# A decoder trunk layer on one core: stick-breaking scores as three products of float32r parts, with the norm weights' load and the squares moved

## The chip, the core and the metric

The kernel runs on one core of one Trainium2 chip. The metric is the device time of one execution in microseconds (us). The time before is 767.2 us, the median of three runs (766.13 to 767.41).

The names below are those of the profile. PE is the matrix engine, and PEld its loading of stationary operands; DVE, ACT and POOL are the vector, scalar and general engines; SP issues transfers. Each engine works through its own instructions strictly in the order in which the program holds them, and waits where an operand is not there yet.

## The reference

One layer with 512 tokens of 1024 features. Two token mixers read the same normalised input: stick-breaking attention (8 heads of 64) and a dilated sliding-window attention (12 heads of 64). Their outputs are projected up, gated, merged and projected out; a SwiGLU block with 2816 hidden features and a final norm follow. All of it is float32.

```python
u = rms_norm(x, norm_mix_g)
q_sb, k_sb, v_sb, q_dl, k_dl, v_dl, gate_sb, gate_dl = split(u @ w_in)
# stick-breaking, per head
z = (q @ k.T) / 8
log_keep  = where(causal, log_sigmoid(-z), 0)
log_after = reverse_cumsum(log_keep) - log_keep
a = where(causal, exp(log_sigmoid(z) + log_after), 0)
o_sb = a @ v
merged = sigmoid(gate_sb) * (o_sb @ w_sb_up) + sigmoid(gate_dl) * (o_dl @ w_dil_up)
x = x + merged @ w_out
u2 = rms_norm(x, norm_ffn_g)
x = x + (silu(g_ff) * up_ff) @ w_ffn_out      # g_ff, up_ff = split(u2 @ w_ffn_in)
out = rms_norm(x, norm_final_g)
```

## The kernel before

Features lie on the partitions and tokens along the free axis. Every large product is made of three: an operand is split into a float32r part (`hi`, a cast on ACT) and what the cast left over (`lo`, a subtraction on DVE), and `mm3` (L157) adds hi by hi, hi by lo and lo by hi into one bank. Weights come in chunks of 128 by 1024 from HBM on SP's queue (`dma_chunk`, L104) into a ring of three `raw` tiles, are split (`split_chunk`, L116) into `whi` and `wlo`, and are used two chunks later. `weights(i, ahead)` (L146) issues the transfers and the splits up to two chunks ahead of the product that asks.

**Start (L197 to L231).** Chunks 0 and 1 (query and key of the first pair of heads) and the eight tiles of x come in pieces, in turn. For each of the eight blocks k, `norm_split` (L175) multiplies x by the norm's weight `gt` on ACT (`xh`) and forms the rest on DVE (`xl`). `gt` is loaded on POOL's queue (L173). The four squares of x (L226) are held behind the last of these splits. The sixteen triples called `first` (L606) use the blocks as they come. Chunk 2 and the three that follow are the values, whose product is `pvvs`; chunk 2 uses blocks 0 and 1 alone.

**Attention.** Projections run on PE one after another; each is evacuated from its bank by DVE (`proj_feature`, L344), which multiplies by the row factors `rb`. There are two banks for projections (tag `proj`), used in turn, so the projection after next waits for the evacuation of this one. The attention's own work is written as generators that advance by ticks, one tick for each triple, and so lies between the projections: `sb_pair` (L412) for the four pairs of stick-breaking heads, with the score tiles `z0x`, `z0y`, `z0z` and so on for pair 0, and `dil_pair` (L507) for the two pairs of dilated heads. The scores of a pair are float32 products over the 64 features of a head, one head on the upper half of the partitions and one on the lower (L417). After the scores come the mask, the exponentials and the products with the values. `split_out` (L397) splits what a pair puts out into `oh` and `ol` tiles: `ohs`, `ols` for stick-breaking heads, `ohd`, `old` for dilated ones.

**What sets the order.** A scheduler that runs while the program is built decides the order on each engine; `tc.high_priority()` raises what lies in it. Tiles of one tag share a ring of buffers, which are handed out in the order in which the program asks for them. Before, the evacuated projections have the tag `qk` (16 buffers), the first four outputs tags of their own, and the two dilated outputs the tag `st` (4 buffers).

**After the attention** come the up projection, the gates (`gs`, `gd`, sixteen projections already made during the attention), the output projection and the SwiGLU block, whose PE order is written by hand. The change doesn't touch them.

Of the kernel before, what the change touches and what calls it, by code (L numbers as in the profile page):

```python
# [10 lines left out]
F32 = mybir.dt.float32  # L11
F32R = mybir.dt.float32r
# [4 lines left out]
P = 128  # L17
# [6 lines left out]
NEG = -(2.0 ** 100)  # L24
NOSYNC = mybir.DependencyInfo(mybir.DependencyClass.NoSync, mybir.DependencyReason.SCHED_ONLY)
BANKS = {"proj": 2, "att": 3}
RAW, NQ, N4, N2, NS = 3, 16, 9, 6, 4

HALVES = [0, 4, 1, 5, 2, 6, 3, 7]

# [13 lines left out]
def trunk_kernel(ctx, tc, xT, gains, w_in, w_up, w_o, w_f, w_d, bias, out):  # L44
# [20 lines left out]
    def bank(tag, name):  # L65
# [3 lines left out]
            return ppool[1].tile([P, S], F32, tag="att" if tag == "alpha" else "sums", name=name, bufs=BANKS["att"])  # L69
        return pair(name)[:, 0, :]  # L70


    warm = cp.tile([P, P], BF16)
    V.memset(warm, 0.0)
# [41 lines left out]
    def split_chunk(i):  # L116
        kind, _, n = chunks[i]
        if i < len(chunks) - 1 and i != first_s4:
            hi = wp.tile([P, 1024], F32R, tag="whi", name=f"whi{i}")
            lo = wp.tile([P, 1024], F32R, tag="wlo", name=f"wlo{i}")  # L120
        else:
            pair_ = wide(f"w{i}", F32R)
            hi, lo = pair_[:, 0, :], pair_[:, 1, :]
        parts[i] = (hi, lo)
        hi, lo = hi[:, :n], lo[:, :n]
        if kind == "plain":
            r = raws.pop(i)[:, :n]
        elif kind == "A1":
            r = raws[i]
        elif kind == "S23":  # L130

            u = raws[i]
            V.tensor_tensor(out=u[:, 0, :], in0=u[:, 1, :], in1=u[:, 2, :], op=ALU.add)
            r = raws["S23"] = wide(f"s23{i}")
            V.tensor_tensor(out=r, in0=u[:, 0:2, :], in1=raws[i - 1][:, :S].unsqueeze(1).to_broadcast([P, 2, S]), op=ALU.add)
        elif kind == "S1":
            r = raws.pop(i - 1)[:, 0:3:2, :]
        else:
            r = fpool[0].tile([P, S], F32, tag="s4", name=f"s4{i}", bufs=1)
            V.tensor_tensor(out=r, in0=raws["S23"][:, 0, :], in1=raws.pop(i - 3)[:, S:], op=ALU.add)  # L140
        if kind in ("S23", "S1"):
            hi, lo = (t.rearrange("p (a n) -> p a n", a=2) for t in (hi, lo))
        A.copy(hi, r)  # L143
        V.tensor_tensor(out=lo, in0=r, in1=hi.bitcast(F32), op=ALU.subtract)  # L144
# [17 lines left out]
    def split_to(hi, lo, src):  # L162
        A.copy(hi, src)
        return V.tensor_tensor(out=lo, in0=src, in1=hi.bitcast(F32), op=ALU.subtract)
# [3 lines left out]
    sqp = ctx.enter_context(tc.tile_pool(name="sqp", bufs=2))  # L168

    fpool = [None]  # L170
    gt = cp.tile([P, 24], F32)
    g32 = cp.tile([P, KD], F32)
    nc.gpsimd.dma_start(out=gt, in_=gains)  # L173

    def norm_split(k, x, gcol, hi, lo):  # L175
        g = gt[:, gcol + k:gcol + k + 1]
        i = A.mul(hi, x, g)
        V.scalar_tensor_tensor(out=lo, in0=x, scalar=g, in1=hi.bitcast(F32), op0=ALU.mult, op1=ALU.subtract)
        return i
# [33 lines left out]
    for k in range(KD):  # L213
        cs = slice(k * P, (k + 2) * P)
        if k % 2 == 0:
            split_to(parts[0][0][:, cs], parts[0][1][:, cs], raws[0][:, cs])
        hi = xp.tile([P, S], F32R, tag=f"xh{k}", name=f"xh{k}")
        lo = xp.tile([P, S], F32R, tag=f"xl{k}", name=f"xl{k}")
        last_split = norm_split(k, xw[k // 2][:, k % 2, :], 0, hi, lo)
        if k % 2 == 0:  # L220
            split_to(parts[1][0][:, cs], parts[1][1][:, cs], raws[1][:, cs])
        xh.append(hi)
        xl.append(lo)
    with tc.high_priority():
        for x in xw:
            i = A.activation(x, x, AF.Square)  # L226
            tc.add_manual_dep(i.ins, last_split.ins.name, NOSYNC, reason="issue order")
        V.tensor_tensor(out=xw[0], in0=xw[0], in1=xw[1], op=ALU.add)
        V.tensor_tensor(out=xw[2], in0=xw[2], in1=xw[3], op=ALU.add)
        V.tensor_tensor(out=xw[0], in0=xw[0], in1=xw[2], op=ALU.add)  # L230
        V.tensor_tensor(out=acc1, in0=xw[0][:, 0, :], in1=xw[0][:, 1, :], op=ALU.add)  # L231
# [109 lines left out]
                with tc.high_priority():  # L341
                    between[k]()

    def proj_feature(name, scale=None, ps=None, blocks=False):  # L344
        if ps is None:
            ps = bank("proj", f"pj{name}")
            product(ps, xh, xl, next_weights(), KD)
        rb = rows["rb"]
        o = ap_.tile([P, S], F32, tag="qk", name=name, bufs=NQ)
        view = (lambda t, out=False: t.rearrange("p (c i) -> p i c" if out else "p (i c) -> p i c", c=4)) if blocks else (lambda t, out=False: t)  # L350
        with tc.high_priority():
            if scale is None:
                V.tensor_tensor(out=view(o, True), in0=view(ps), in1=view(rb), op=ALU.mult)
            else:
                V.scalar_tensor_tensor(out=view(o, True), in0=view(ps), scalar=scale, in1=view(rb), op0=ALU.mult, op1=ALU.mult)
        return o

    def proj_token(name, kind, wide_, pairs=0):
# [36 lines left out]
    o_hi, o_lo = {}, {}  # L395

    def split_out(i, name, src):  # L397
        if i < 4:
            hi = ap_.tile([P, S], F32R, tag=f"oh{name}", name=f"oh{name}")
            lo = ap_.tile([P, S], F32R, tag=f"ol{name}", name=f"ol{name}")  # L400
        else:
            hi, lo = (ap_.tile([P, S], F32R, tag="st", name=f"o{t}{name}", bufs=NS) for t in "hl")
        split_to(hi, lo, src)
        o_hi[i], o_lo[i] = hi, lo

# [6 lines left out]
    def sb_pair(n, q, k, v, hb, done):  # L412
        def scores(name, parts):
            ps = take(f"z{n}{name}")
            for i, (a, o) in enumerate(parts):
                for h in range(2):
                    T.matmul(ps[:, h, o:o + S - a * P], k[hs[h], a * P:(a + 1) * P], q[hs[h], a * P:], start=i == 0, stop=False, skip_group_check=True)  # L417
            for h in range(2):
                diag = ps[:, h, :].rearrange("p (a b) -> p a b", b=P)
                diag = diag[:, 0:4:3, :] if len(parts) == 2 else diag[:, 0:1, :]  # L420
                T.matmul(diag, idb, mask[:, :len(parts)], start=False, stop=False, skip_group_check=True)
            return ps
# [165 lines left out]
            yield from dil_pair(n, [vals[f"dq{n}{g}"] for g in range(3)], [vals[f"dk{n}{g}"] for g in range(3)], lambda: vals.get("vd"))  # L588

    def project(n):  # L590
        vals[f"q{n}"] = proj_feature(f"sq{n}", 0.125)
        vals[f"k{n}"] = proj_feature(f"sk{n}")

    def project_dil(n):
        for g in range(3):
# [12 lines left out]
    def first_steps():  # L608
        yield from row_steps()
        give(3)  # L610
        vals["q0"] = proj_feature("sq0", 0.125, first[0])
        vals["k0"] = proj_feature("sk0", None, first[1])

    start(first_steps(), 10)
    start(sb_all())
# [384 lines left out]
```

## Time and profile before

| what | before |
|---|---|
| median of three runs | 767.2 us (766.13 to 767.41) |
| the profiled execution | 768.07 us |
| its span, first to last instruction | 766.4 us |
| granted PE clock, mean over the span | 0.995 |
| DVE busy | 511.6 us (67%) |
| ACT busy | 358.6 us (47%) |
| POOL busy | 29.0 us (4%) |
| HBM read | 71.32 MB |

The profiled execution lies 0.87 us above the median of the runs, and its span is 1.67 us shorter than its own time. Rows of the timeline read: start in us, duration in us, engine, line, operation, written tile, read tiles, shapes, count, and in brackets the idle time of that engine just before the row with what ended it. A float32r matmul over 512 columns is shown as 0.39 us long, but the next one starts 0.23 us after it, since they overlap; so starts count on PE, not durations.

### The profile page before, as it was taken

How to read it: one execution, taken by the hardware profiler on the slowest of the kernel's cores; microseconds unless marked ns; L12 is line 12 of the kernel's file. 1: busy time of each engine (PE TensorE's matmuls, PEld its weight loads, DVE VectorE, ACT ScalarE, POOL GpSimd, SP SyncE). 2: the span in 40 equal slices, each digit the busy share in tenths (PEclk: the TensorE clock that was granted, in tenths of full speed). 3: DMA queues.
4: the chain of work that ended last, by engine and by line, in shares of the span. 5: the costliest groups of instructions: out<-in, count | busy, mean ns of one | idle time of the engine just before them, and what ended most of it. 6: DMA issues, size and time to landing. Idle time of an engine off the chain costs nothing. (4 is left out here: it accounts for less than half of the span.)

```text
span 766.4 us, 11025 instructions
## 1 busy us (share of the span) xinstructions
PE 753.4 (98%) x4498; PEld 646.6 (84%) x4498; DVE 511.6 (67%) x685; ACT 358.6 (47%) x509; POOL 29.0 (4%) x38
## 2 busy tenths in 40 slices
PE   8999999999999999999999999999999999999996
PEld 5877767798887878888788999999999999999985
DVE  6454646344677775358698989877788777776643
ACT  7273727462233352333455666544445454444453
POOL 1000000000101100000000100000000000000032
PEclk9999999999999999999999999999999999999998
DMA  7312121123224223233432223323333323332113
GB/s 247 137 56 83 56 83 56 56 69 124 83 83 159 88 84 103 62 91 129 145 103 79 75 89 103 103 79 122 98 106 114 103 82 113 100 105 77 56 55 111
DMA packets 24947, 74.13 MB, mean 97 GB/s; under 512 B 2736, under 2 KB 5824, under 8 KB 24768
## 3 DMA queue, kind: packets, MB, share of 16 engines
q1 hardware_dynamic: 23664, 69.87, 28.3%
q0 software_dynamic: 816, 3.16, 1.3%
q8 instruction: 35, 0.57, 0.3%
q10 hardware_dynamic: 416, 0.39, 0.2%
q14 instruction: 16, 0.13, 0.1%
HBM read 71.32 MB, written 2.10 MB: 96 GB/s over the span
## 5 line engine op out<-in xcount | busy, mean ns | idle before, releaser
L143 ACT CAST whi<-raw 128x1024 fp32r<-128x1024 f32 (+2 forms) x113 | 108.5, 962 | 160.8 <-issue 49.2
L144 DVE TENSOR_TENSOR wlo<-raw,whi 128x1024 fp32r<-128x1024 f32 (+2 forms) x113 | 125.9, 1115 | 34.4 <-ACT whi L143 33.6
L756 PE MATMUL pf<-fh,whi 128*128 128x256 f32 x348 | 98.8, 284 | 0.4 <-ACT q L763 0.3
L758 PE MATMUL pf<-fh,wlo 128*128 128x256 f32 x348 | 98.5, 283 | 0.0
L757 PE MATMUL pf<-fl,whi 128*128 128x256 f32 x348 | 98.5, 283 | 0.0
L756 PE MATMUL pg<-fh,whi 128*128 128x256 f32 x264 | 75.1, 285 | 0.6 <-ACT q L763 0.6
L757 PE MATMUL pg<-fl,whi 128*128 128x256 f32 x264 | 74.7, 283 | 0.0
L758 PE MATMUL pg<-fh,wlo 128*128 128x256 f32 x264 | 74.7, 283 | 0.0
L756 PEld LDWEIGHTS pf<-fh,whi 128*128 128x128 f32 x348 | 66.7, 192 | 1.5 <-ACT q L763 0.8
L757 PEld LDWEIGHTS pf<-fl,whi 128*128 128x128 f32 x348 | 66.7, 192 | 0.6
L758 PEld LDWEIGHTS pf<-fh,wlo 128*128 128x128 f32 x348 | 66.7, 192 | 0.3 <-DVE wlo L144 0.2
L144 DVE TENSOR_TENSOR wlo<-s,whi 128x1024 fp32r<-128x1024 f32 (+1 forms) x43 | 41.3, 960 | 15.9 <-ACT whi L143 15.7
L756 PEld LDWEIGHTS pg<-fh,whi 128*128 128x128 f32 x264 | 50.6, 192 | 1.1 <-ACT q L763 0.8
L143 ACT CAST whi<-s 128x1024 fp32r<-128x1024 f32 (+1 forms) x43 | 36.2, 841 | 32.6 <-PE pg L757 20.5
L757 PEld LDWEIGHTS pg<-fl,whi 128*128 128x128 f32 x264 | 50.7, 192 | 0.0
L758 PEld LDWEIGHTS pg<-fh,wlo 128*128 128x128 f32 x264 | 50.6, 192 | 0.0
L158 PE MATMUL pd<-hh,whi 128*128 128x512 f32 (+1 forms) x132 | 50.4, 382 | 0.0
L159 PE MATMUL pd<-hl,whi 128*128 128x512 f32 (+1 forms) x132 | 50.3, 381 | 0.0
L160 PE MATMUL pd<-hh,wlo 128*128 128x512 f32 (+1 forms) x132 | 50.1, 379 | 0.0
L143 ACT CAST whi<-rawu 128x1024 fp32r<-128x1024 f32 x22 | 23.1, 1051 | 28.4 <-PE pd L159 23.7
L853 DVE TENSOR_TENSOR res<-pd,res 128x512 f32<-128x512 f32 (+1 forms) x36 | 22.6, 629 | 19.5 <-PE pd L160 19.3
L160 PEld LDWEIGHTS pd<-hh,wlo 128*128 128x128 f32 x132 | 24.8, 188 | 4.8
(469 smaller groups left out, 1741.4 us busy)
## 6 DMA issues: line engine op xcount, KB each, us to landing
raw<-in_w_in_dram SPq DMA_DIRECT2D x44, 512.0 KB, 3.3
rawu<-in_w_ffn_in_dram SPq DMA_DIRECT2D x22, 512.0 KB, 3.3
raw<-in_w_ffn_in_dram SPq DMA_DIRECT2D x22, 512.0 KB, 3.4
raw<-in_w_ffn_out_dram SPq DMA_DIRECT2D x24, 384.0 KB, 3.2
raw<-in_w_out_dram SPq DMA_DIRECT2D x8, 512.0 KB, 3.3
raw<-in_w_up_dram SPq DMA_DIRECT2D x8, 384.0 KB, 3.0
x<-in_xT_dram SPq DMA_DIRECT2D x8, 256.0 KB, 4.6
res<-in_xT_dram POOLq DMA_DIRECT2D x8, 256.0 KB, 3.6
```

The source lines that it names most:

```text
L143: A.copy(hi, r)
L144: V.tensor_tensor(out=lo, in0=r, in1=hi.bitcast(F32), op=ALU.subtract)
L158: T.matmul(ps, shi, mhi, start=first, stop=False)
L159: T.matmul(ps, shi, mlo, start=False, stop=False)
L160: T.matmul(ps, slo, mhi, start=False, stop=last)
L756: T.matmul(ps, hi[:, cs], xhi, start=first and k == 0, stop=False, skip_group_check=True)
L757: T.matmul(ps, hi[:, cs], xlo, start=False, stop=False, skip_group_check=True)
L758: T.matmul(ps, lo[:, cs], xhi, start=False, stop=last and k == 3, skip_group_check=True)
L853: V.tensor_tensor(out=x, in0=ps, in1=x, op=ALU.add)
```

## The change

Five things change.

1. `proj_feature(split=True)` for the stick-breaking q and k: DVE evacuates into a tile of a new ring `raw2` (2 buffers), ACT casts it into a hi tile and DVE makes the lo tile; both are float32r and have the tag `qk`.
2. The scores become three float32r products per head, k hi by q hi, k hi by q lo, k lo by q hi, in place of one float32 product.
3. The ring `qk` has 28 buffers instead of 16, and all outputs of `split_out` come from it too.
4. `gt` is loaded first of all, on ACT's queue.
5. `weights(0)` is called ahead of the squares, so that chunks 2 (and what belongs to it) are issued and split with high priority there, and the squares follow the split of chunk 2, no longer the last split of x.

```diff
-RAW, NQ, N4, N2, NS = 3, 16, 9, 6, 4
+RAW, NQ, N4, N2 = 3, 28, 9, 6
...
+    gt = cp.tile([P, 24], F32)
+    nc.scalar.dma_start(out=gt, in_=gains)
...
-        A.copy(hi, r)
+        state["last"] = A.copy(hi, r)
...
-    gt = cp.tile([P, 24], F32)
     g32 = cp.tile([P, KD], F32)
-    nc.gpsimd.dma_start(out=gt, in_=gains)
...
     with tc.high_priority():
+        weights(0)
         for x in xw:
             i = A.activation(x, x, AF.Square)
-            tc.add_manual_dep(i.ins, last_split.ins.name, NOSYNC, reason="issue order")
+            tc.add_manual_dep(i.ins, state["last"].ins.name, NOSYNC, reason="issue order")
...
-    def proj_feature(name, scale=None, ps=None, blocks=False):
+    def proj_feature(name, scale=None, ps=None, blocks=False, split=False):
...
-        o = ap_.tile([P, S], F32, tag="qk", name=name, bufs=NQ)
+        o = ap_.tile([P, S], F32, tag="raw2" if split else "qk", name=name, bufs=2 if split else NQ)
...
+            if split:
+                hi, lo = (ap_.tile([P, S], F32R, tag="qk", name=f"{t}{name}", bufs=NQ) for t in "hl")
+                split_to(hi, lo, o)
+                return hi, lo
...
     def split_out(i, name, src):
-        if i < 4:
-            hi = ap_.tile([P, S], F32R, tag=f"oh{name}", name=f"oh{name}")
-            lo = ap_.tile([P, S], F32R, tag=f"ol{name}", name=f"ol{name}")
-        else:
-            hi, lo = (ap_.tile([P, S], F32R, tag="st", name=f"o{t}{name}", bufs=NS) for t in "hl")
+        hi, lo = (ap_.tile([P, S], F32R, tag="qk", name=f"o{t}{name}", bufs=NQ) for t in "hl")
...
             for i, (a, o) in enumerate(parts):
-                for h in range(2):
-                    T.matmul(ps[:, h, o:o + S - a * P], k[hs[h], a * P:(a + 1) * P], q[hs[h], a * P:], start=i == 0, stop=False, skip_group_check=True)
+                for j, (x, y) in enumerate(((0, 0), (0, 1), (1, 0))):
+                    for h in range(2):
+                        T.matmul(ps[:, h, o:o + S - a * P], k[x][hs[h], a * P:(a + 1) * P], q[y][hs[h], a * P:], start=i == 0 and j == 0, stop=False, skip_group_check=True)
```

The calls of `proj_feature` for `sq` and `sk` (in `project` and `first_steps`) pass `split=True`; nothing else is changed. Three places show what this does to the order.

**SP's queue at the start.** `raw_170` is chunk 2; `raw_96`, `raw_99` are pieces of chunks 0 and 1, and `x_103`, `x_108` hold two blocks of x each. Before:

```order
L207 DMA raw_96<-in_w_in_dram 128x256
L210 DMA x_103<-in_xT_dram 128x512
L207 DMA raw_99<-in_w_in_dram 128x256
L212 DMA x_103<-in_xT_dram 128x512
L207 DMA raw_96<-in_w_in_dram 128x256
L210 DMA x_108<-in_xT_dram 128x512
```

And now:

```order
L207 DMA raw_96<-in_w_in_dram 128x256
L210 DMA x_103<-in_xT_dram 128x512
L207 DMA raw_99<-in_w_in_dram 128x256
L113 DMA raw_170<-in_w_in_dram 128x1024
L212 DMA x_103<-in_xT_dram 128x512
L207 DMA raw_96<-in_w_in_dram 128x256
```

Chunk 2 (512 KB) has moved ahead of block 1 of x; chunk 3 likewise stands ahead of block 6. On ACT and DVE, the split of chunk 2 stands ahead of the split of block 1. On PE the 24 matmuls of chunk 2, which stood behind all 48 of `first`, now lie between them, from the seventh matmul on:

```order
L162 MATMUL first<-xh_124,wlo_101 128x512
L160 MATMUL pvvs_259<-whi_176,xh_124 128x512
L160 MATMUL pvvs_260<-whi_176,xh_124 128x512
L160 MATMUL pvvs_261<-whi_176,xh_124 128x512
L160 MATMUL first<-xh_130,whi_97 128x512
L161 MATMUL pvvs_259<-wlo_177,xh_124 128x512
L162 MATMUL pvvs_259<-whi_176,xl_125 128x512
```

**DVE at the end of dilated pair 0.** `dk` is the evacuation of the last key projection, `rl`, `nt` belong to the pair's output, `old` is the lo part of that output, and `p<-d` is the first step of pair 1. Before:

```order
L353 TENSOR_TENSOR dk_1726<-pjdk_1650,rb_354 128x128x4
L558 RECIPROCAL rl_1715<-dl_1712 128x512
L144 TENSOR_TENSOR wlo_1732<-raw_1618,whi_1731 128x1024
L561 TENSOR_TENSOR nt_1719<-n_1678,nb_1716 128x512
L562 TENSOR_TENSOR rl_1715<-nt_1719,rl_1715 128x512
L519 TENSOR_TENSOR p_1762<-d_1753,bt 128x1024
L164 TENSOR_TENSOR old_1723<-rl_1715,ohd_1722 128x512
L353 TENSOR_TENSOR gs_1770<-pjgs_1728,rb_354 128x512
```

And now:

```order
L560 RECIPROCAL rl_1811<-dl_1808 128x512
L146 TENSOR_TENSOR wlo_1828<-raw_1714,whi_1827 128x1024
L563 TENSOR_TENSOR nt_1815<-n_1774,nb_1812 128x512
L564 TENSOR_TENSOR rl_1811<-nt_1815,rl_1811 128x512
L521 TENSOR_TENSOR p_1858<-d_1849,bt 128x1024
L166 TENSOR_TENSOR old_1819<-rl_1811,ohd_1818 128x512
L354 TENSOR_TENSOR dk_1822<-pjdk_1746,rb_354 128x128x4
L354 TENSOR_TENSOR gs_1866<-pjgs_1824,rb_354 128x512
```

The evacuation `dk` has moved from ahead of the reciprocal to behind `old`. Its tile comes from the ring `qk`, in which `ohd_1818` and `old_1819` are now asked for just before `dk_1822`.

**DVE at the end of dilated pair 1.** `gd` and `gs` are evacuations of the gate projections `pjgd` and `pjgs`. Before:

```order
L353 TENSOR_TENSOR gd_2094<-pjgd_2018,rb_354 128x512
L558 RECIPROCAL rl_2083<-dl_2080 128x512
L144 TENSOR_TENSOR wlo_2100<-raw_1986,whi_2099 128x1024
L561 TENSOR_TENSOR nt_2087<-n_2046,nb_2084 128x512
L562 TENSOR_TENSOR rl_2083<-nt_2087,rl_2083 128x512
L353 TENSOR_TENSOR gs_2127<-pjgs_2096,rb_354 128x512
L144 TENSOR_TENSOR wlo_2133<-raw_2019,whi_2132 128x1024
L164 TENSOR_TENSOR old_2091<-rl_2083,ohd_2090 128x512
L353 TENSOR_TENSOR gd_2160<-pjgd_2129,rb_354 128x512
```

And now:

```order
L560 RECIPROCAL rl_2179<-dl_2176 128x512
L146 TENSOR_TENSOR wlo_2196<-raw_2082,whi_2195 128x1024
L563 TENSOR_TENSOR nt_2183<-n_2142,nb_2180 128x512
L564 TENSOR_TENSOR rl_2179<-nt_2183,rl_2179 128x512
L146 TENSOR_TENSOR wlo_2229<-raw_2115,whi_2228 128x1024
L166 TENSOR_TENSOR old_2187<-rl_2179,ohd_2186 128x512
L354 TENSOR_TENSOR gd_2190<-pjgd_2114,rb_354 128x512
L354 TENSOR_TENSOR gs_2223<-pjgs_2192,rb_354 128x512
```

Here too an evacuation, `gd_2190` of the projection `pjgd_2114`, has moved from ahead of the reciprocal to behind `old`, and `gs_2223` behind it. On PE the projection after next, `pjgd_2225`, is to use the bank of `pjgd_2114`; at the place before, `pjgd_1868` is to use that of `pjdk_1746`.

More of the change, by code (lines that the diff above doesn't have):

```diff
@@ L218, in trunk_kernel @@
         lo = xp.tile([P, S], F32R, tag=f"xl{k}", name=f"xl{k}")
-        last_split = norm_split(k, xw[k // 2][:, k % 2, :], 0, hi, lo)
+        norm_split(k, xw[k // 2][:, k % 2, :], 0, hi, lo)
         if k % 2 == 0:
@@ L590, in project @@
     def project(n):
-        vals[f"q{n}"] = proj_feature(f"sq{n}", 0.125)
-        vals[f"k{n}"] = proj_feature(f"sk{n}")
+        vals[f"q{n}"] = proj_feature(f"sq{n}", 0.125, split=True)
+        vals[f"k{n}"] = proj_feature(f"sk{n}", split=True)
     def project_dil(n):
@@ L610, in first_steps @@
         give(3)
-        vals["q0"] = proj_feature("sq0", 0.125, first[0])
-        vals["k0"] = proj_feature("sk0", None, first[1])
+        vals["q0"] = proj_feature("sq0", 0.125, first[0], split=True)
+        vals["k0"] = proj_feature("sk0", None, first[1], split=True)
     start(first_steps(), 10)
```

## The prediction

> **What bounds the kernel now.** I read the busy times first, then PE's timeline for the places where its starts are further apart than the work asks for.
>
> ```profile
> PE 753.4 (98%) x4498; PEld 646.6 (84%) x4498; DVE 511.6 (67%) x685; ACT 358.6 (47%) x509; POOL 29.0 (4%) x38
> ...
> 500.09 0.39 PE L160 MATMUL pd<-hh,wlo 128*128 128x512 f32 x1
> 500.32 0.28 PE L756 MATMUL pf<-fh,whi 128*128 128x256 f32 x1
> 500.43 0.28 PE L757 MATMUL pf<-fl,whi 128*128 128x256 f32 x1
> 500.55 0.28 PE L758 MATMUL pf<-fh,wlo 128*128 128x256 f32 x1
> ```
>
> PE is the bound: 98% of the span. Its stream sets the pace, a float32r matmul of 512 columns every 0.227 us and one of 256 every 0.12 us. So each edit counts for what it adds to or takes from PE's stream: its own matmuls, and the time in which PE stands. DVE and ACT have room (67% and 47%), and work there costs only where PE waits for it.
>
> **Part 1, the scores.** First the rows of pair 0, then the group of `z0z` (duration, first and last start):
>
> ```profile
> 45.84 1.14 PE L417 MATMUL z0x<-sq,sk 64*128 64x384 f32 x8
> 46.91 0.39 PE L421 MATMUL z0x<-mask,idb 128*128 128x256 bf16 x2
> 47.23 0.70 PE L417 MATMUL z0y<-sq,sk 64*128 64x256 f32 x4
> 47.87 0.28 PE L421 MATMUL z0y<-mask,idb 128*128 128x128 bf16 x2
> ...
> 50.90 1.13 PE L417 MATMUL z0z<-sq,sk 64*128 64x512 f32 x4
> 51.96 0.29 PE L421 MATMUL z0z<-mask,idb 128*128 128x128 bf16 x2
> L417 PE MATMUL z0z<-sq,sk x4: 589/641/693, 50.9 to 51.4; 64*128 64x512 f32 x4
> ```
>
> From score to mask, pair 0 takes 1.07 us for x (384 and 128 columns), 0.64 for y (256) and 1.06 for z (512). All three fit 0.2 us, which I read as loads and changes of shape that stay, and 0.85 for 512 columns of both heads. Each float32 matmul is two records; the last of z's four starts at 51.4, half-way, so the heads run in pairs (one after the other the last would start at 51.7). Three float32r products at 0.227 give 0.68 instead of 0.85: z gains 0.17. For y, 3 x 0.12 = 0.36 against 0.43: 0.07. For x, 384 columns at 0.17 (between the two intervals above) make 0.51 against 0.64, but the 128 columns cannot go below a load of some 0.11 a product, 0.33 against 0.21: x gains about 0.02. A pair gains 0.26, four pairs 1.0 to 1.1. I take **-1.1 us**. No row shows a float32r matmul below 256 columns; between the load (0.11) and twice that (the float32 pace of 128 columns, four passes), the 12 products of 128 columns cost nothing more or 1.3 us more in all. I take the first, since the load is the nearest row, and keep both ends.
>
> The added splits are eight casts and eight subtractions of 128x512:
>
> ```profile
> L163 ACT CAST ohs<-o 128x512 fp32r<-128x512 f32 x4 | 2.5, 619 | 5.1 <-DVE o L492 5.1
> L164 DVE TENSOR_TENSOR ols<-o,ohs 128x512 fp32r<-128x512 f32 x4 | 2.8, 690 | 2.2 <-ACT ohs L163 2.2
> ```
>
> That is 5.0 us on ACT and 5.5 on DVE, spread over some 100 us, and PE's stream hides it: in the new order pair 0's scores have moved 15 matmuls (3.4 us) further back, which covers cast and subtraction (1.3 us, and two queues). Pair 1 has the least cover, 6 matmuls and four value products, about 3 us. I cost it at nothing; without cover a pair would wait about 1.3 us, 5 us in all.
>
> **Part 2, the start.**
>
> ```profile
> 4.63 0.72 ACT L177 ACTIVATE xh<-x,gt 128x512 fp32r<-128x512 f32 x1 [0.86 <-DMA gt<-in_gains_dram]
> 6.44 0.72 ACT L177 ACTIVATE xh<-x,gt 128x512 fp32r<-128x512 f32 x1 [0.79 <-DMA x<-in_xT_dram]
> 17.10 1.03 ACT L143 CAST whi<-raw 128x1024 fp32r<-128x1024 f32 x1
> 17.22 0.39 PE L160 MATMUL first<-xh,wlo 128*128 128x512 f32 x1
> 18.16 1.23 DVE L144 TENSOR_TENSOR wlo<-raw,whi 128x1024 fp32r<-128x1024 f32 x1 [0.66 <-ACT whi L143]
> 18.18 0.97 PE L158 MATMUL pvvs<-whi,xh 128*128 128x512 f32 x3 [0.57 <-ACT whi L143]
> 19.44 0.50 PE L159 MATMUL pvvs<-wlo,xh 128*128 128x512 f32 x1 [0.29 <-DVE wlo L144]
> 24.33 0.84 PE L158 MATMUL pvvs<-whi,xh 128*128 128x512 f32 x3
> 12.00:13.00 1.00, 1.00 (x6) 0.83 (x5) 1.00 (x3) 0.99 (x2) 0.00 (x0) 1.00 0.89 356
> ```
>
> Before, the squares held chunk 2's cast until 17.10, and PE stood for it: `first` ends at 17.22 + 0.23 = 17.45, chunk 2's 24 matmuls would end 24 x 0.227 = 5.45 later, at 22.90, and chunk 3 begins at 24.33, so 1.4 us were lost. Those waits go. But chunk 2 now comes ahead of block 1 of x, and 512 KB at the 356 GB/s of the window row take 1.47 us. Block 1 landed by 6.44, with its own 256 KB (0.74) behind chunk 2, so chunk 2 lands at about 5.7 + 1.47 = 7.17. Then ACT's cast (1.03) ends at 8.2, DVE's subtraction (1.23) at 9.45, and PE, which has ten matmuls to do before that one (six of block 0, four more), runs on from 9.45. Behind it stand 72 - 10 = 62 matmuls to the first of chunk 3: 62 x 0.227 = 14.1, which is 23.5 against 24.33. I take **-0.8 us**. If chunk 2 lands at 6.0 it is -1.9; if the blocks behind chunk 3, 1.5 us later again, reach PE late, up to +0.5 (they have cover: block 7 comes some 3 us later than before and PE asks for it 5 us later). `gt` earlier frees block 0 sooner (its row waited 0.86 us for it), but PE then waits for chunk 2 instead: nothing. POOL loses an issue it had time for; SP's queue, past which chunks 2 and 3 moved, is in the sum; the squares now lie between the splits, and the row sums need them only 20 matmuls into chunk 3.
>
> **Part 3, two evacuations behind the split of an output.** This is the largest term, and the diff hides it in a tag. `old` and `dk` now come from one ring, handed out in the program's order, and DVE's queue has `dk` behind `old`.
>
> ```profile
> 229.73 1.08 PE L555 MATMUL dl<-mb,ones 128*64 128x512 f32 x4
> 229.84 1.07 DVE L353 TENSOR_TENSOR dk<-pjdk,rb 128x512 f32<-128x512 f32 x1 [4.30 <-PE pjdk L160]
> 230.86 3.36 DVE L558 RECIPROCAL rl<-dl 128x512 f32<-128x512 f32 x1
> ...
> 238.03 0.68 DVE L164 TENSOR_TENSOR old<-rl,ohd 128x512 fp32r<-128x512 f32 x1
> 238.63 0.69 DVE L353 TENSOR_TENSOR gs<-pjgs,rb 128x512 f32<-128x512 f32 x1
> 237.65 0.39 PE L158 MATMUL pjgd<-xh,whi 128*128 128x512 f32 x1
> ```
>
> The reciprocal cannot start sooner without `dk` ahead of it, since `dl` ends at 229.73 + 1.08 = 230.81. So the chain stays where it is, `dk` takes the slot at 238.63 and ends at 239.70, and `pjgd`, which needs its bank and began at 237.65, begins at 239.75: **+2.1 us**.
>
> ```profile
> 284.92 3.36 DVE L558 RECIPROCAL rl<-dl 128x512 f32<-128x512 f32 x1 [0.33 <-PE dl L555]
> ...
> 290.99 0.68 DVE L353 TENSOR_TENSOR gs<-pjgs,rb 128x512 f32<-128x512 f32 x1
> 291.59 1.22 DVE L144 TENSOR_TENSOR wlo<-raw,whi 128x1024 fp32r<-128x1024 f32 x1
> 292.73 0.68 DVE L164 TENSOR_TENSOR old<-rl,ohd 128x512 fp32r<-128x512 f32 x1
> 290.41 1.06 ACT L143 CAST whi<-raw 128x1024 fp32r<-128x1024 f32 x1 [5.12 <-issue]
> 290.39 0.39 PE L158 MATMUL pjgd<-xh,whi 128*128 128x512 f32 x1
> ```
>
> Here `wlo` waits for ACT's cast, which ends at 290.41 + 1.06 = 291.47 whatever `gs` does, so moving `gs` behind saves 0.1 us only: `old` at 292.63, `gd` at 293.25 to 293.95, and the `pjgd` that began at 290.39 begins at 293.95: **+3.5 us**. Queued behind on DVE are `gs` and the next `wlo`; PE asks for both one projection later (24 x 0.227 = 5.4 us), so nothing is added there. PE has no idle time later that gives this back.
>
> **Part 4, the clock after such a stop.**
>
> ```profile
> 29.09 2.81 PE L264 MATMUL rows<-ones,acc 128*128 128x1 f32 x16
> 31.00:32.00 1.00, 1.00 (x5) 0.64 0.00 0
> 32.00:33.00 1.00, 1.00 (x3) 0.50 0.00 0
> 33.00:34.00 1.00, 1.00 (x3) 0.50 0.00 0
> 34.00:35.00 1.00, 1.00 (x4) 0.66 0.00 0
> ```
>
> PE's granted clock (the second number after the count) fell to half behind 2.8 us of matmuls one column wide: 0.36 + 0.50 + 0.50 + 0.34 = 1.7 us of full-speed work lost. A stop of 3.5 us is longer than that weak stretch, so I expect one such drop behind it: **+1.7 us**. The stop of 2.1 us is shorter; I take none there, with 1.7 as its other end. The Trainium skill's page "TensorE: Matmul & The Clock Gate" (Part 1) says that the clock falls after at least one idle window of about 3.4 us, that these windows run free, and that gaps under that are safe. By that rule the 3.5 us stop would hold a whole window hardly ever, and the sum would be 1.7 us lower. The trace speaks against the strict form, for the drop at 31 us came behind 2.8 us that were not even idle, while its length agrees.
>
> **Sum.** -1.1 - 0.8 + 2.1 + 3.5 + 1.7 = +5.4 us on the profiled execution's 768.07, which is 773.5 there (span 771.8). That execution lay 0.87 us above the median, so the median of runs should be **772.6 us**, +0.7%. About 0.2% (1.5 us) is what a measurement of this kernel can tell from no change.
>
> **The rivals.**
>
> - No drop of the clock, the skill's rule in its strict form. The stop is idle and not weak work, which is one row's evidence only; then +3.7, 770.9 us. Chance 0.25.
> - The products over 128 columns run at half the pace or worse: +1.3 on the forecast, 773.9 us. Nothing in the trace speaks either way. Chance 0.12.
> - The change doesn't do what it says on PE: two heads of float32r do not overlap. Then z costs 6 x 0.227 = 1.36 for 0.85, x about 1.68 for 0.85, y 0.72 for 0.43, together +1.6 a pair, +6.5 in all in place of -1.1: 780.2 us. All float32 pairs in the trace overlap, against it. Chance 0.05.
> - Not slower: the start gives more. From 5.40 (the first matmul) to 24.33 PE had 72 x 0.227 = 16.3 us of work, so 2.6 us are idle there, and `gt` could give 0.4 before that. If chunk 2 lands before block 0's six matmuls are done (about 6.4), PE never waits for it, and the start gives up to 3.0. With no drop of the clock: 5.6 - 1.1 - 3.0 = +1.5, 768.7 us, at the edge of no change. Against it stands the transfer of 1.47 us, which is only that short if nothing else is on its way. Chance 0.08.
>
> **How the numbers follow.** The forecast has 0.50, the rivals 0.25, 0.12, 0.05 and 0.08. The range of 8 in 10 takes in the first two rivals and the ends of the start (-1.1 and +1.3 about the value taken) and a drop behind the shorter stop: 768.8 to 776.0 us. Faster by over 0.2% would need the best start, no drop, and shorter stops as well: 0.03. Within 0.2%: 0.08. Slower: 0.89.
>
> **What would show it.** In the profile after: PE rows of the first `pjgd` and of the one behind the second `dl` with 2 and 3.5 us idle, put down to DVE `dk` and `gd`; those rows on DVE right behind `old`; the half clock in the windows behind them; the first matmul of chunk 3 at about 23.5; from `z0z` to its mask 0.9 us. The prediction is wrong if the two evacuations find another way to a free bank, if the opening is far from 23.5, or if a third wait stands in the attention, say scores waiting for their lo parts.

## The result, and the profile after

The changed kernel takes 773.78 us (median of six runs, 773.02 to 775.40) against 767.7 of the kernel before beside it (766.13 to 769.58): a ratio of 1.0082, 95% interval 1.0065 to 1.0099. It is slower by about 6.1 us; the forecast was 772.6 us, 5.4 us slower. The profiled execution has a span of 772.1 us (766.4 before) and a mean granted clock of 0.994 (0.995).

The page of the changed kernel, the line of busy times and one group (columns as before; behind the bar stands the engine's idle time ahead of the group and what ended most of it):

```profile
PE 755.3 (98%) x4530; PEld 650.7 (84%) x4530; DVE 516.1 (67%) x693; ACT 361.8 (47%) x517; POOL 28.3 (4%) x37
...
L160 PE MATMUL pjgd<-xh,whi 128*128 128x512 f32 x64 | 26.0, 407 | 5.5 <-DVE gd L354 3.5
```

PE is still "98% busy". What was lost shows in the second line alone: 5.5 us of idle time ahead of one group, put down to DVE's evacuations. The group did not stand on the page before.

The timeline of the changed kernel, PE's rows at the start and around the first two scores:

```profile
9.39 0.47 PE L161 MATMUL pvvs<-wlo,xh 128*128 128x512 f32 x1
...
23.30 0.39 PE L162 MATMUL first<-xh,wlo 128*128 128x512 f32 x1
23.53 0.84 PE L160 MATMUL pvvs<-whi,xh 128*128 128x512 f32 x3
...
47.04 0.45 PE L419 MATMUL z0x<-hsq,hsk 64*128 64x384 f32 x2
...
48.05 0.39 PE L423 MATMUL z0x<-mask,idb 128*128 128x256 bf16 x2
...
49.13 0.50 PE L419 MATMUL z0z<-hsq,hsk 64*128 64x512 f32 x2
...
50.03 0.29 PE L423 MATMUL z0z<-mask,idb 128*128 128x128 bf16 x2
```

The first product with chunk 2's lo part starts at 9.39 (9.45 was forecast), and chunk 3's first product at 23.53, 0.80 us earlier than before (24.33). From score to mask, x takes 1.01 us (1.07 before) and z 0.90 (1.06); the heads overlap, and the products over 128 columns are not slow.

DVE's and PE's rows at the first stop:

```profile
229.24 3.36 DVE L560 RECIPROCAL rl<-dl 128x512 f32<-128x512 f32 x1 [5.33 <-PE dl L557]
...
236.41 0.68 DVE L166 TENSOR_TENSOR old<-rl,ohd 128x512 fp32r<-128x512 f32 x1
237.00 1.03 DVE L354 TENSOR_TENSOR dk<-pjdk,rb 128x512 f32<-128x512 f32 x1
235.79 0.40 PE L162 MATMUL pjgs<-xh,wlo 128*128 128x512 f32 x1
238.18 0.47 PE L160 MATMUL pjgd<-xh,whi 128*128 128x512 f32 x1 [1.99 <-DVE dk L354]
```

And at the second, with the windows behind it (length, PE busy, granted clock, share of the DMA engines, GB/s):

```profile
293.26 0.68 DVE L166 TENSOR_TENSOR old<-rl,ohd 128x512 fp32r<-128x512 f32 x1
293.86 0.68 DVE L354 TENSOR_TENSOR gd<-pjgd,rb 128x512 f32<-128x512 f32 x1
290.79 0.39 PE L162 MATMUL pjgs<-xh,wlo 128*128 128x512 f32 x1
294.69 0.47 PE L160 MATMUL pjgd<-xh,whi 128*128 128x512 f32 x1 [3.51 <-DVE gd L354]
```

```profile
295.00:296.00 1.00, 1.00 (x5) 0.80 0.88 320
296.00:297.00 1.00, 1.00 (x3) 0.50 0.11 45
...
298.00:299.00 1.00, 1.00 (x4) 0.50 0.00 0
```

`dk` and `gd` stand right behind `old`, as the forecast read from the order, and PE waits for each: 238.18 - 235.79 = 2.39 between starts that are 0.23 apart otherwise, and 294.69 - 290.79 = 3.90. The clock is at one half from 295.6 (0.80 over the window from 295) to 299.0.

Marks on PE (the start of the last matmul of a product, after minus before) show where the time went:

| stretch on PE | forecast | measured | late by then |
|---|---|---|---|
| start, to chunk 3's first product | -0.8 | -0.80 | -0.80 |
| half clock behind `rows` (the eight one-column products that sum the squares) at 31 us, in the execution before and not in this one | none | -1.40 | -2.20 |
| attention, last `pvvs` to first `pjgs` | -1.1 | +0.58 | -1.62 |
| first stop | +2.1 | +2.25 | +0.63 |
| second stop and the half clock behind it | +3.5 and +1.7 | +5.40 | +6.03 |
| output projection, to the last `po` | none | -1.21 | +4.82 |
| the rest | none | +0.56 | +5.38 |

Three rows, with four terms of the sum, came as forecast. The attention row did not, by 1.68 us; and two differences that have no part in the sum make up for it: a half clock of the execution before that did not recur, and a shorter wait in the output projection, put down to DVE's additions to the residual `res`, 1.43 us before and 0.24 after:

```profile
373.58 0.50 PE L158 MATMUL po<-mh,whi 128*128 128x512 f32 x1 [1.43 <-DVE res L717]
```

```profile
378.42 0.50 PE L160 MATMUL po<-mh,whi 128*128 128x512 f32 x1 [0.24 <-DVE res L719]
```

In the first run below, which has no stops, the stretch from the last `up` to the last `po` is as short (44.22 us, 44.31 as changed, 45.52 before). So it is not the time of the stops that is given back here; why the wait shrank was not looked into.

### The profile page after: what moved, and what is told of

It is laid out like the page before. It is cut to its first block, busy times and chain, and to the rows that moved or that the text cites. A ratio compares the mean times of both kernels' runs of the same rounds, so it can differ in the third digit from the quotient of the medians.

```text
span 772.1 us, 11101 instructions
## 1 busy us (share of the span) xinstructions
PE 755.3 (98%) x4530; PEld 650.7 (84%) x4530; DVE 516.1 (67%) x693; ACT 361.8 (47%) x517; POOL 28.3 (4%) x37
## 4 chain that ended last, share of the span: by engine, by line
PE 73%; issue 23%; DVE 1%; DMA 1%; ACT 1%; POOL 0%; SPq 0%; POOLq 0%; DVEq 0%; ACTq 0%
PE pd L160 5%; PE pd L161 5%; PE pd L162 5%; PE pf L758 5%; PE pf L759 5%; PE pf L760 5%; PE pg L758 4%; PE pg L760 4%; PE pg L759 4%; PE pvvd L160 2%; PE pjdk L160 2%; PE pjdq L160 2%; PE pvvd L162 2%; PE pjdq L162 1%; PE pvvd L161 1%
## 5 line engine op out<-in xcount | busy, mean ns | idle before, releaser
L160 PE MATMUL pjgd<-xh,whi 128*128 128x512 f32 x64 | 26.0, 407 | 5.5 <-DVE gd L354 3.5
```

The costliest lines, as they stand in the source:

```text
L160: T.matmul(ps, shi, mhi, start=first, stop=False)
```

## The experiments

All times are medians beside runs of the kernel before on the same chip. The median of these was 767.3 us beside the runs of parts 1, 2 and 4, 766.65 beside the first three of part 3 and 767.33 beside its last. There are twelve runs; one of them is the changed kernel again. Brackets hold the lowest and the highest time, the ratio to the kernel before and its 95% interval.

### 1. Is it the ring? Three runs

The dilated outputs get a ring of their own again, first both, then that of pair 0 alone, then that of pair 1 alone; everything else stays as changed.

```diff
-RAW, NQ, N4, N2 = 3, 28, 9, 6
+RAW, NQ, N4, N2 = 3, 24, 9, 6
...
-        hi, lo = (ap_.tile([P, S], F32R, tag="qk", name=f"o{t}{name}", bufs=NQ) for t in "hl")
+        own = i >= 4
+        hi, lo = (ap_.tile([P, S], F32R, tag="st" if own else "qk", name=f"o{t}{name}", bufs=4 if own else NQ) for t in "hl")
```

In the other two `own` is `i == 4` or `i == 5`, with two buffers in the own ring and 26 in `qk`.

> The changed kernel, with the two outputs of the dilated pairs (old, ohd) back in a ring of their own of 4 buffers, and the ring of q, k, gates and stick-breaking outputs at 24, so that the memory is the same. DVE's queue then has dk and gd ahead of the reciprocals again. Ring theory (the two evacuations behind the split of an output are the loss): both stops (2.2 and 3.7 us) and the half clock behind the second (1.7) go, 7.6 us less than the changed kernel's 773.8: 766.2 us, at or a little below the kernel before. Rival (the loss is in the attention's scores and their added splits): the time stays within 2 us of 773.8.

> The changed kernel, with the output of dilated pair 0 alone in a ring of its own (2 buffers, the shared ring at 26). Only dk is ahead of its reciprocal again. Ring theory: the first stop (2.2 us, 2.38 between two starts on PE) goes, the second (3.7) and the half clock behind it (1.7) stay: 771.6 us. If the half clock is set by the two stops together, it goes too: 769.9. Rival (the two stops are one delay, and the first only moves the second): the second stop grows by what the first loses, 773.8.

> The changed kernel, with the output of dilated pair 1 alone in a ring of its own (2 buffers, the shared ring at 26). Only gd is ahead of its reciprocal again. Ring theory: the second stop (3.7 us) and the half clock behind it (1.7) go, the first (2.2) stays, with full clock behind it: 768.4 us. If a stop of 2.2 us is enough for a drop of the clock: 770.1.

Measured: both 766.29 us (765.33 to 767.22, ratio 0.9984, interval 0.9975 to 0.9994); pair 0 alone 772.13 (1.0056, 1.0043 to 1.0069); pair 1 alone 769.07 (1.0024, 1.0013 to 1.0035). With the own ring for both, DVE's rows of the timeline are those of before again:

```profile
228.17 1.07 DVE L354 TENSOR_TENSOR dk<-pjdk,rb 128x512 f32<-128x512 f32 x1 [4.29 <-PE pjdk L162]
229.19 3.36 DVE L561 RECIPROCAL rl<-dl 128x512 f32<-128x512 f32 x1
...
289.32 0.68 DVE L354 TENSOR_TENSOR gs<-pjgs,rb 128x512 f32<-128x512 f32 x1
...
291.06 0.69 DVE L166 TENSOR_TENSOR old<-rl,ohd 128x512 fp32r<-128x512 f32 x1
```

`dk` is ahead of the reciprocal and `gs` ahead of `old`, no `pjgd` waits, and the time is 7.5 us below the changed kernel's. So the whole loss, and a little more, comes with the shared tag (part 3 narrows this down). It is the change without its loss, about 1 us faster than before. With an own ring for one pair alone, the stop that is left has its old length in the trace (3.5 us of idle time put down to `gd`, 2.0 put down to `dk`), so neither stop moves the other. The times are 772.1 us where 771.6 was expected, and 769.1, between the 768.4 and 770.1 of the two cases. In the latter run the executions differ by their granted clock: six have 0.998 (mean 768.2 us), three 0.996 (769.7) and two 0.993 (770.9).

### 2. The clock behind a stop: three runs with work in the stops

Zeros' matmuls in bfloat16 go ahead of the waiting `pjgd`, into the unused half of the bank of `dl` (`spare`); the stop stays, but PE is busy in it. First 12 in the second stop (`f == 4` alone), then 9 in the first as well, then float32r products of the normed input's parts in place of the zeros.

```diff
         gs.append(proj_feature(f"gs{f}"))
+        if f in (0, 4):
+            for _ in range(12 if f else 9):
+                T.matmul(vals["spare"], warm, warm.unsqueeze(1).to_broadcast([P, 4, P]), start=True, stop=True, skip_group_check=True)
         gd.append(proj_feature(f"gd{f}"))
```

> The changed kernel, with 12 matmuls of zeros (bf16, 512 columns, into a bank that nobody reads) on PE just ahead of the projection that waits in the second stop, about 2.6 us of work inside 3.7 us of waiting. Clock theory (1.7 us of the loss is the half clock that follows an idle PE): the wait ends at the same time, but no half clock follows: 772.1 us. Rival (the half clock comes by chance, or zeros do not hold it): 773.8, and the windows behind the stop show half the clock again.

> The changed kernel with bfloat16 matmuls of zeros ahead of both waiting products (9 ahead of the first gd product, 12 ahead of the fifth), written to the unused half of the denominators' bank; the waits stay, TensorE is busy in them. Theory A, half clock follows a 3.41 us window of a fixed raster in which TensorE was busy less than about 45% of the time: no half clock behind either stop, granted clock of 0.997 or 0.998 in all runs, 1.7 to 2.4 us below the changed kernel: 771.4 to 772.1 us. Rival B, matmuls of zeros do not hold the clock: half clock behind a stop in the profile, 773.8. Rival C, the half clock costs nothing at the end since something else is late by then: no half clock behind the stops and 773.8.

> As the run before it, with float32r products of the normed input's own parts (128x512, data that are not zero) in place of the zeros. Theory A: the same as with zeros, 771.4 to 772.1 us. Rival B (zeros do not hold the clock): here 771.4 to 772.1, with zeros 773.8. Rival C: 773.8 in both.

Measured: 773.92 us (772.62 to 775.37, 1.0084, 1.0071 to 1.0096); 773.33 (772.37 to 776.35, 1.0088, 1.0070 to 1.0105); 773.62 (773.35 to 774.26, 1.0088, 1.0074 to 1.0103). None is faster, so by their times the rivals at 773.8 came out three times. The traces say more. Windows of the run with work in the second stop alone, cut at the moment the clock changed:

```profile
235.34:238.75 3.41, 1.47 (x6) 1.00 0.43 154
238.75:242.16 3.41, 3.37 (x8) 0.50 0.23 70
```

The half clock left the second stop and came behind the first, where PE had been busy for 1.47 of 3.41 us (43%). With work in both stops, PE's rows at the second and the windows there:

```profile
294.66 0.39 PE L162 MATMUL pjgs<-xh,wlo 128*128 128x512 f32 x1
294.89 2.76 PE L635 MATMUL dl<-warm 128*128 128x512 bf16 x12
298.55 0.47 PE L160 MATMUL pjgd<-xh,whi 128*128 128x512 f32 x1 [0.90 <-DVE gd L354]
```

```profile
298.00:300.00 2.00, 1.45 (x6) 1.00 0.76 262
300.00:302.00 2.00, 2.00 (x10) 1.00 0.00 0
```

The stop has its old length (298.55 - 294.66 = 3.89), and no half clock follows. With data in place of zeros the same holds. But both profiled executions have a half clock behind `rows` instead, at 33.1 and 31.4 us, which that of the changed kernel had not. The one with zeros has one more, right after its start, behind a window in which PE waited 1.57 us for ACT:

```profile
5.75:9.17 3.42, 1.77 (x7) 1.00 0.85 291
9.17:12.58 3.41, 3.41 (x9) 0.50 0.99 337
```

To price the clock apart from that, take in each trace the stretch from the last start of `pvvd` to the last start of `up`, which holds both stops and nothing of the start:

| kernel | stops | half clocks in the stretch | us | over before |
|---|---|---|---|---|
| before | none | 0 | 170.77 | |
| own ring for both | none | 0 | 170.96 | 0.19 |
| own ring for pair 1 | first | 0 | 173.18 | 2.41 |
| own ring for pair 0 | second | 1 | 176.31 | 5.54 |
| work in both stops, zeros | both | 0 | 177.04 | 6.27 |
| work in both stops, data | both | 0 | 177.05 | 6.28 |
| work in the second stop | both | 1 | 178.52 | 7.75 |
| as changed | both | 1 | 178.60 | 7.83 |
| as changed, again (next part) | both | 2 | 180.11 | 9.34 |

The rows add up with three prices: first stop 2.41 - 0.19 = 2.2, second 6.27 - 2.41 = 3.9, a half clock 1.5 each (7.83 - 6.27 = 1.56; 9.34 - 6.27 = 3.07 for two).

### 3. Where else the clock falls: the changed kernel again, and `rows` spread out

The changed kernel once more. Then the run with the own ring, with the eight one-column products of `rows`, which stand in one block of some 2.4 us, placed one behind each of eight steps of the value product. Then that spread in the changed kernel with its shared ring and with work in both stops. Last, the spread in the kernel before.

```diff
-        with tc.high_priority():
-            rows["r1"] = row_factors(acc1, 8, "1", p[:, 0, :])
-        yield 7
+        for j in range(8):
+            with tc.high_priority():
+                r1 = row_factors(acc1, 8, "1", p[:, 0, :], j)
+            yield 1
+        rows["r1"] = r1
+        yield 4
...
-    start(first_steps(), 10)
+    start(first_steps(), 14)
```

With `j` given, `row_factors` issues that product alone, ordered behind the latest step of the value product.

> The changed kernel itself once more, beside the runs below: 773.8 us, granted clock 0.994 or 0.995. If half clock comes where a window of the 3.41 us raster is mostly idle, it stands behind the second stop (3.7 us idle) in this profile too, wherever the raster begins; behind the one-column products (rows) and the first stop (2.2 us) only if the raster falls so.

> The run with the own ring, and the one-column products (rows, 2.2 us in one block) put one behind each of eight steps of the value product. Theory: the block of one-column products is what halves the clock in about half of all executions, of the kernel before too; spread, all executions have a granted clock of 0.997 or 0.998 and the time is that of the faster half, 765.3 to 766.0 us (own ring alone: 766.3). Rival: the two clock levels come from elsewhere and stay, 766.3 to 766.8.

> The changed kernel with zeros' matmuls in both stops, and the one-column products spread as above: the stops stay and no place is left where half clock was seen. Theory A (the clock term of 1.7 us is real, the fillers alone did not show it since half of the executions lost it again behind rows): 771.2 to 772.2 us, granted clock 0.997 or 0.998 in all. Rival: fillers gain nothing at the end, 773.3 to 773.8 at whatever clock.

> The kernel before (float32 scores, old start, own ring as it had) with the one-column products spread one behind each step: all executions at a granted clock of 0.997 or 0.998, so the start and the split scores are compared with the same spread run of the changed kernel with its own ring (764.7) without the two clock levels. By the forecast's terms (start 0.8, scores 1.1) it is 1.9 us slower than that: 766.6. By the start alone, the scores bringing nothing at the end: 765.5. By the attention of the changed kernel's profile (scores cost 0.6): 764.9. If the two clock levels do not come from the one-column products, this kernel shows both, as before does.

**Changed again:** 773.51 us (772.94 to 776.44; 1.0087, 1.0067 to 1.0108). The profiled execution is the slowest of these, 776.44. Its windows:

```profile
32.00:33.00 1.00, 1.00 (x4) 0.58 0.00 0
33.00:34.00 1.00, 1.00 (x3) 0.50 0.00 0
...
35.00:36.00 1.00, 1.00 (x5) 0.71 0.63 164
...
240.00:242.00 2.00, 2.00 (x6) 0.59 0.00 0
...
298.00:300.00 2.00, 2.00 (x6) 0.60 0.57 227
```

The clock fell behind `rows` and behind both stops. The means give the moments: 0.58 over 32 to 33 is full speed for 0.16 us, so it fell at 32.16; in the same way at 240.36 and 298.40. The distances are 208.2 and 58.0 us, 61 and 17 times 3.41, and each drop lasts 3.4 us. So the clock is decided on a raster of 3.41 us that runs through the whole execution. In the changed kernel's first profile a window of the raster cut the first stop in two, and PE was busy for 2.02 of 3.41 us in the one that held most of it; no half clock came. In the run with the own ring for pair 1 it was 1.62 of 3.41 (47%), and none came:

```profile
234.61:238.02 3.41, 1.62 (x8) 1.00 0.48 156
238.02:241.43 3.41, 3.21 (x25) 1.00 0.20 62
```

**Own ring, `rows` spread:** 764.74 us (763.88 to 765.47; ratio 0.9968, 0.9958 to 0.9978), below the 765.3 to 766.0 expected and the fastest of all. All twelve executions have a granted clock of 0.997 to 0.999. By that alone they would be about as fast as the six executions of the own ring that have 0.997 or 0.998 (mean 765.8 us). Much of the rest lies in the order of the attention: from the last `pvvs` to the last `up` PE takes 314.96 us in place of 315.94. Of 82 executions of the kernel before beside these runs, 41 have 0.997 or 0.998 (mean 766.4 us) and 41 have 0.994 to 0.996 (mean 767.9): 1.5 us apart, as the table has it for one half clock. PE's rows with the spread:

```profile
29.79 0.28 PE L265 MATMUL rows<-ones,acc 128*128 128x1 f32 x2
...
30.47 0.39 PE L162 MATMUL pvvs<-whi,xl 128*128 128x512 f32 x1
30.70 0.28 PE L265 MATMUL rows<-ones,acc 128*128 128x1 f32 x2
```

**Before, `rows` spread:** 767.11 us (766.57 to 769.03; 0.9997, 0.9988 to 1.0006), and again all twelve at 0.997 to 0.999. So the block of one-column products is what divides the executions. But the spread alone brings this kernel nothing in the median: its executions lie 0.7 us above those of the kernel before that have the same clock (767.1 against 766.4). The row factors come later by it and the attention is placed anew (its first score starts at 50.58, 4.7 us later, but 4.1 later in the run above as well, which gained). Its trace puts the loss in the attention: from the last `pvvs` to the last `up` PE takes 316.41 us in place of 315.36 (part 4 says in which groups). Why the new places cost that here and gained in the run above was not tried.

**Changed, spread, work in both stops:** 769.41 us (768.65 to 769.92; 1.0029, 1.0019 to 1.0039), some 2 us below what was expected, and for a reason that the expectation had wrong. DVE's rows, then PE's at the second place:

```profile
224.23 1.10 DVE L361 TENSOR_TENSOR dk<-pjdk,rb 128x512 f32<-128x512 f32 x1 [1.08 <-PE pjdk L162]
...
229.36 3.36 DVE L569 RECIPROCAL rl<-dl 128x512 f32<-128x512 f32 x1 [2.98 <-PE dl L566]
293.09 0.39 PE L161 MATMUL pjgd<-xl,whi 128*128 128x512 f32 x1
293.32 2.76 PE L642 MATMUL dl<-warm 128*128 128x512 bf16 x12
295.73 0.58 PE L162 MATMUL pjgd<-xh,wlo 128*128 128x512 f32 x1
```

The stops are gone, though the ring is shared, for `dk` is evacuated 5 us ahead of the reciprocal. The numbers of the tiles rise in the order in which the program asks for them. In the changed kernel's order `dk_1822` stands right behind `old_1819`; here it is

```order
L361 TENSOR_TENSOR dk_1808<-pjdk_1746,rb_387 128x128x4
L569 RECIPROCAL rl_1823<-dl_1820 128x512
...
L166 TENSOR_TENSOR old_1831<-rl_1823,ohd_1830 128x512
```

The spread moved the output by some ticks, and it is now asked for behind `dk` (1830 and 1808) where it was asked for just ahead of it (1818 and 1822). The fillers now stand in the midst of a running product and are pure cost: 21 of them, some 0.22 us each, 4.6 us, and 769.41 - 764.74 = 4.67. This run therefore says nothing of the clock's price. It does say that the stops hang on the order in which output and evacuation are asked for, not on the ring as such.

### 4. The two gains by themselves

The start alone (the kernel before with `gt` on ACT's queue, `weights(0)` ahead of the squares, and no other edit), and the scores alone (the run with the own ring, with the old start).

```diff
-    gt = cp.tile([P, 24], F32)
-    nc.scalar.dma_start(out=gt, in_=gains)
...
-        weights(0)
...
-            tc.add_manual_dep(i.ins, state["last"].ins.name, NOSYNC, reason="issue order")
+            tc.add_manual_dep(i.ins, last_split.ins.name, NOSYNC, reason="issue order")
```

(This is the second edit; the first is its reverse on the kernel before.)

> The kernel before with the new start alone: the norms' weights on ScalarE's queue, the third weight chunk split ahead of the squares. Theory: chunk 3's first product at 23.5 us as in the changed kernel, and the 0.8 us stay to the end: 766.5 us against 767.3 before. Rival: the 0.8 us are lost again at the next wait (rows), 767.3.

> The changed kernel with the dilated outputs' parts in a ring of their own (so without the stops) and with the old start: what the split scores cost or bring by themselves. By the forecast's term for the scores: 1.1 us below before, 766.2 us. By the attention of the changed kernel's profile as a whole (0.58 us longer, the products shorter but pairs of heads parted by projections): 0.6 above, 767.9. If both the start (0.8) and the scores add up to the run with the own ring and the new start (766.3), this one comes out at 767.1.

Measured: the start 766.39 us (765.44 to 767.90; 0.9996, 0.9986 to 1.0006), the scores 766.74 (765.33 to 767.61; 0.9994, 0.9983 to 1.0005). The medians are 0.9 and 0.6 us lower, the intervals include no change: two clock levels 1.5 us apart blur what is smaller. Among executions with a granted clock of 0.997 or 0.998 the start has a mean of 765.96 us (eight) and the scores 766.15 (seven), against 766.11 of the kernel before beside them (eleven): neither shows by itself. The cleanest comparison is that of the two runs with `rows` spread, where all executions have one level: 0.9968 with the change and its own ring, 0.9997 without, 0.29% or 2.2 us for start and scores together (forecast 1.9). It is not clean either: the spread by itself cost the kernel before some 0.7 us, and the order in the attention differs. From last `pvvs` to first `pjgs` PE takes 183.64 and 185.08 us; of these 1.44 us, 0.86 are the score products, and the rest lies in the matmuls around them.

Why the attention did not get shorter shows in one group, of the kernel before and of the changed one (duration min, median, max; first and last start):

```profile
L446 PE MATMUL b<-t0x,ones x8: 272/380/537, 68.3 to 69.1; 128*64 128x384 f32 x4, 128*64 128x128 f32 x4
```

```profile
L448 PE MATMUL b<-t0x,ones x8: 273/404/537, 68.2 to 70.5; 128*64 128x384 f32 x4, 128*64 128x128 f32 x4
```

Before, the eight records run through in 0.8 us, two heads at a time. In the changed order matmuls of `z0z` and of `a` stand between them, and some heads run without their partner:

```profile
69.00 0.74 PE L441 MATMUL z0z<-l0z,tri 128*128 128x512 f32 x2
69.66 0.54 PE L448 MATMUL b<-t0x,ones 128*64 128x384 f32 x3
...
70.04 0.49 PE L448 MATMUL b<-t0x,ones 128*64 128x384 f32 x1
```

Counted from start to start, the score products with their masks take 0.80 us less over the attention, while `b` takes 0.54 more, `d` 0.42, `a` 0.25, the matmuls with `tri` 0.22. With the own ring for both, and in the run of the scores alone, these are nearly the same as here. The run of the start alone, with the old scores, has all these at their old values. But where the order moves they move with the old scores too: in the kernel before with `rows` spread `b` takes 0.74 us more than before, `tri` 0.44 and `a` 0.40. So an order can cost this without the new form of the products. That the parted pairs are the cause is read from the traces; no run keeps the pairs together and all else as changed, so it is not shown by itself.

## Why the prediction was right, and where it was not

**The stops** (+2.1, +3.5) were right in place, cause and size: the traces give 2.2 and 3.9 by the stretch, the row they are put down to is `dk` and `gd`, and an own ring takes them away one by one.

**The clock** (+1.7) was right in the trace and its mechanism was too simple. A half clock did follow the second stop, at 1.5 to 1.7 us. But what decides is the share of busy time in a window of the raster, not the length of the gap: the step "the stop of 2.1 us is shorter; I take none there" holds in some executions only. The rival by the strict rule of the Trainium skill's page "TensorE: Matmul & The Clock Gate" (Part 1: windows of some 3.4 us that run free, a drop after one that is idle) is right in raster and length: 3.41 us, 61 and 17 whole windows apart. It is wrong in the condition: the clock fell behind windows in which PE was busy for 43%. The timed runs bear out its price in one place: with the own ring for pair 1, the executions at 0.998, 0.996 and 0.993 lie 1.5 and 1.3 us apart (768.2, 769.7 and 770.9). They do not show the gain from work in the stops: those medians (773.3 to 773.9) lie within 0.5 us of the changed kernel's two (773.5 and 773.8). A half clock of 3.41 us takes 0.002 off the mean clock, and eight of the eleven executions with work in both stops have 0.993 to 0.996 (0.997 to 0.999 in all with `rows` spread), so by this reading they still had one somewhere, as the two profiled ones had behind `rows`; the other three, at 0.998, took 772.4, 772.7 and 773.6. Whether half clocks behind `rows` are more frequent in these kernels, or came by chance, stays open.

**The start** (-0.8) was right on PE, in the moment at which it runs on (9.39 for 9.45) and at chunk 3 (23.53 for 23.5); in the time of the run by itself it cannot be told from nothing.

**The scores** (-1.1) are the step that failed. In pair 0 the products are as short as forecast: 1.07 to 1.01, 0.64 to 0.55 and 1.06 to 0.90 make 0.31, 1.2 in four such pairs; over all four the group takes 0.80 less, 0.3 short of the term. The added splits are hidden, as forecast: the profile shows no wait of PE in the attention, before or after. Wrong was that the term held the score products alone and put the rest of PE's stream at nothing. The order changed where the attention's matmuls lie between the projections, and the matmuls around the scores, by the traces with heads parted from their partners, took 1.4 us back, so the attention became 0.58 us longer. In the two kernels with `rows` spread, which have other orders again, the same stretch is 1.44 us shorter with the split scores; so the term hangs on the order. I counted the instructions whose form changed, and not those whose neighbours changed.

**The sum** came out within 0.7 us (5.4 against 6.1 between the medians) partly by luck: in the profile a half clock that did not recur (1.4) and a shorter wait in the output projection (1.2) balanced the scores' miss of 1.7 us, 0.6 in the last part of the kernel and 0.35 by which the stops were longer than forecast. The shift of 0.87 from the profiled execution to the median was right in kind: that execution had the half clock behind `rows`, and the median lies between the two levels.

## What to carry to other kernels

Before a tile is given another tag, look up what else is handed out from that ring near the end of a long chain: here a shared ring put two evacuations behind a reciprocal's chain, and 2.2 and 3.9 us of PE's time with them, where the engines' busy shares showed nothing. Where a matmul's form changes inside an order made by a scheduler, count the matmuls around it again, too. And where executions of a kernel fall into two groups, look for a block of weak matrix work, here 2.4 us beside a window of 3.41. Spread out, it left one group in both kernels; but the spread moves the order too, and only with the own ring did the time gain by it (764.74 us, the best here).

## What the runs showed of the hardware

- The granted clock is decided on a raster of 3.41 us. It fell for one window behind windows in which the profile has PE busy for 0%, 14%, 27%, 42% and 43% (the two stops, over all traces in which they were idle), and not behind 47% and 59%. The border is not sharp in this measure: at the start of the run with zeros in both stops it fell behind 52%.
- A busy PE in the profile is not enough to hold the clock: in the changed kernel's second profile, as in the kernel before, it fell behind one-column products that the profile shows as 100% busy. Zeros of 512 columns, on the other hand, held it as well as data. That work counts by what it streams is a reading of this.
- Where the raster begins differs between executions, so the same stop costs 2.2 us in one and 3.7 in the next.
